# Attention scores: K's low part against Q's high part alone, in passes of 64 rows

## The chip, the cores and the metric

The kernel runs on one core of one Trainium2 chip. The metric is the device time of one execution in microseconds (us); a comparison goes by the median of several executions. TensorE (PE in the profile) multiplies a stationary operand of up to 128 rows and 128 columns, which a load of weights (PEld) puts into its array, with a moving operand that streams through; the rows are the dimension that is summed over. VectorE (DVE), ScalarE (ACT), GpSimd (POOL) and the issuing queue SyncE (SP) work beside it.

## The reference

One step of a hybrid encoder: 1024 prompt tokens and 32 sample tokens of width 1024 go through one layer with a recurrent mixer, then through one layer of sliding-window attention with 16 query heads, 4 key/value heads of 64 dimensions and a learned sink for each head. Only the scores of the second layer are touched by the change:

```python
kb, vb = band(k), band(v)                     # chunks of 64: this one and the two before
s = jnp.einsum('bnqkgd,bnskd->bnkgqs', qb, kb).astype(jnp.float32) * scale
p = sink_softmax(s, sink)                     # max with the sink, exp, divide by the sum
o = jnp.einsum('bnkgqs,bnskd->bnqkgd', p.astype(vb.dtype), vb)
```

All is float32. Outputs are the two streams' activations, the convolution and recurrent states, and K and V rows.

## The kernel before, in words

**High and low parts.** Every product is made from operands that are split into a high part, rounded to the format that TensorE multiplies in one pass (`F32R`), and a low part, the remainder (`split`, L124). Most products are then three passes, high by high, high by low and low by high (`mm3`, L161; `mm3_steps`, L753). The low-by-low product is left out there.

**Scores.** A head has 64 dimensions, so for the scores both parts fit in 128 rows. `q_block` (L905) makes Q of four heads (a group) for a third of the tokens (n = 0, 1, 2: 384, 384 and 288 tokens): `rope` gives the two halves of the dimensions, `halves` splits them into four quarters (high a, high b, low a, low b, 32 rows for each head), they go to `qscr` in device memory and come back as the tile `QU`. Its rows are 32 dimensions each, in the order high a, high b, low a, low b: rows 0-63 hold Q's high part and rows 64-127 its low part, for each of the four heads side by side. `load_kv` (L931) fills `KU` from `kscr`: in `KU[:, 0]` K's high part stands twice, in rows 0-63 and again in rows 64-127, and in `KU[:, 1]` its low part, twice as well. A score block of one head (128 tokens by 256 keys) is therefore two passes of 128 rows: with K's high part, which gives high by high plus low by high, and with K's low part, which gives high by low plus low by low.

**Stages.** For each group g (0 to 3) and each block j of 128 tokens (0 to 7 for the prompt, 8 for the sample) the attention runs in four steps. `stage_s` (L960) makes the scores of four heads in two PSUM banks, two heads in each, and brings them through the mask, the maximum and the exponential into the tile `P` (VectorE at L986, ScalarE at L989). `stage_n` (L993) divides by the sums, `stage_t` (L1003) transposes `P` on TensorE and splits it, and `stage_o` (L1014) multiplies with V (L1019). The loop at L1119 calls `stage_s` of block j+1, `stage_t` of j, `stage_n` of j+1, then six steps of a generator with other products, and `stage_o` of j. These fillers (`fillers`, L1050) are the gate projections `gB` of the group, the Q blocks `rAq` and `rBq` of the next group and, in the last group, the first third of the output projection `obm`.

**What sets the order.** The framework's scheduler orders each engine's instructions by a timing model of its own and by priorities, not strictly as they are written; `pin` marks an instruction that keeps its place in the written order against other marked ones, while unmarked ones can still move in between. Each engine then runs its list in order. Transfers of Q, K, V and weights are issued on SP's queue, in the order of that list as well. In the attention there are three banks for fillers, two for scores (`S`), two for transposes (`T`) and one for `O`.

Of the kernel before, what the change touches and what calls it, by code (L numbers as in the profile page):

```python
# [9 lines left out]
F32 = mybir.dt.float32  # L10
# [7 lines left out]
P = 128  # L18
# [10 lines left out]
NSB = [(0, 384), (384, 768), (768, TOK)]  # L29
# [46 lines left out]
def _trunk(ctx, tc, nc, A):  # L76
    V, S, G = nc.vector, nc.scalar, nc.gpsimd
# [13 lines left out]
    def pin(i, on=True):  # L91
        return tc.keep_in_program_order(i) if on else i

    def bank(name, tag="mm", bufs=None):
        return psum.tile([P, 512], F32, tag=tag, name=name, bufs=bufs or nbank)
# [384 lines left out]
    half = {}  # L480
# [140 lines left out]
    for n in range(3):  # L621
        for m in LATE:
            w = NSB[n][1] - NSB[n][0]
            hl = [late.tile([P, 384], F32R, tag="t", bufs=NT, name=f"y{x}{m}_{n}")[:, :w] for x in "hl"]
# [86 lines left out]
    for n, order in enumerate(orders):  # L711
        zs, acc = {}, []
        w = NSB[n][1] - NSB[n][0]
# [22 lines left out]
    qscr = dram.tile([4, 4, P, TOK], F32, name="qscr")  # L736
    ogscr = dram.tile([6, P, TOK], F32, name="ogscr")

    def att_tile(name, shape, dt, tag, bufs):
        return att.tile([P] + shape, dt, tag=tag, bufs=bufs, name=name)  # L740
# [21 lines left out]
    def rope(n, wA, wB, nm, norm=None):  # L762

        c0, c1 = NSB[n]
        w = c1 - c0
        pa_, pb_ = bank(f"rA{nm}")[:, :w], bank(f"rB{nm}")[:, :w]
        yield from mm3_steps(pa_, wA, x1_of(c0, c1))
        yield
        yield from mm3_steps(pb_, wB, x1_of(c0, c1))
        if norm is not None:  # L770
            norm()
        t = [unit(f"rp{i}{nm}", w=w) for i in range(4)]
        for i, (p, tab) in enumerate(((pa_, cos), (pb_, sin), (pb_, cos), (pa_, sin))):
            V.tensor_tensor(t[i], p, tab[:, c0:c1], op=ALU.mult)
        G.tensor_tensor(t[0], t[0], t[1], op=ALU.subtract)
        G.tensor_tensor(t[2], t[2], t[3], op=ALU.add)
        rope_out[nm] = (t[0], t[2])
        yield
# [7 lines left out]
    def halves(nm, a, b, w):  # L786
        q = quad(f"quad{nm}")
        for i, x in enumerate((a, b)):
            split(q[:, i, :w], q[:, 2 + i, :w], x)
        return q  # L790
# [112 lines left out]
    QU, KU, VU, SG, TT = {}, {}, {}, {}, {}  # L903

    def q_block(g, n):  # L905
        nm = f"q{g}_{n}"
        c0, c1 = NSB[n]
        w = c1 - c0
        yield from rope(n, wts[f"qA{g}"], wts[f"qB{g}"], nm)
        a, b = rope_out.pop(nm)  # L910
        q = halves(nm, a, b, w)
        nc.sync.dma_start(qscr[g].rearrange("x p c -> p x c")[:, :, c0:c1], q[:, :, :w].bitcast(F32))
        QU[g, n] = att_tile(f"Q{g}_{n}", [4, 384], F32R, "Q", 3)
        if n == 2:
            QS[g] = att_tile(f"QS{g}", [4, DEC], F32R, "QS", 2)
        for x in range(4):
            nc.sync.dma_start(QU[g, n][32 * x:32 * x + 32, :, :w].bitcast(F32),
                              qscr[g, x].rearrange("(h d) c -> d h c", h=4)[:, :, c0:c1])
            if n == 2:
                nc.sync.dma_start(QS[g][32 * x:32 * x + 32].bitcast(F32),  # L920
                                  qscr[g, x].rearrange("(h d) c -> d h c", h=4)[:, :, SEQ:])
# [9 lines left out]
    def load_kv(g, n):  # L931
        KU[g, n] = att_tile(f"K{g}_{n}", [2, 640], F32R, "K", 2)
        VU[g, n] = att_tile(f"V{g}_{n}", [5, 128], F32R, "V", 2)
        w = KB1[n] - KB0[n]
        for dup in range(2):
            for half in range(2):
                p0 = dup * 64 + half * 32
                pin(nc.sync.dma_start(KU[g, n][p0:p0 + 32, :, :w].bitcast(F32),
                                      kscr.rearrange("(l f) p c -> p l f c", l=2)[32 * g:32 * g + 32, :, half, KB0[n]:KB1[n]]),
                    g == 0 and n > 0)  # L940
        t0, t1 = KB0[n] // P, KB1[n] // P
        nc.sync.dma_start(VU[g, n][:, :t1 - t0, :].bitcast(F32),
                            vscr.rearrange("t p c -> p t c")[:, t0:t1, g * 128:g * 128 + 128])
# [14 lines left out]
    QS = {}  # L958

    def stage_s(g, j):  # L960

        smp = j == 8
        n = 2 if smp else j // 3
        if (g, n) not in KU:
            load_kv(g, n)
        nm = f"{g}_{j}"
        nh, nk = (1 if smp else 4), (1 if j == 0 else 2)
        t0 = 3 if smp else max(j - 1, 0) - KB0[n] // P
        w = nk * P
        ks = slice(t0 * P, t0 * P + 256)  # L970
        sm = att_tile(f"sm{nm}", [3, 4], F32, "sm", 4)
        nmax, rsum, rl = (sm[:, i, :nh] for i in range(3))
        sk = slice(16 + g, 17 + g) if smp else slice(4 * g, 4 * g + 4)
        msk = smask if smp else mask[:, 256 - w:]

        pt = att_tile(f"P{nm}", [4, 258], F32, "P", 2)
        S.activation(pt[:, :nh, w:w + 1], nsnk[:, sk].unsqueeze(2), AF.Copy)
        for h0 in range(0, nh, 2):
            sb = bank(f"S{nm}_{h0}", "S", 2)
            for h in range(h0, min(h0 + 2, nh)):  # L980
                q = QS[g].rearrange("p h c -> p (h c)") if smp else QU[g, n][:, h, P * j - NSB[n][0]:P * j - NSB[n][0] + P]
                s = sb[:, (h - h0) * 256:(h - h0) * 256 + 256]
                for hl in range(2):
                    pin(nc.tensor.matmul(s, q, KU[g, n][:, hl, ks], start=hl == 0, stop=hl == 1), g == 0 and j == 0)  # L984
            for h in range(h0, min(h0 + 2, nh)):
                V.tensor_tensor_reduce(pt[:, h, :w], sb[:, (h - h0) * 256:(h - h0) * 256 + w], msk,  # L986
                                       -0.125, nsnk[:, sk][:, h:h + 1], op0=ALU.add, op1=ALU.min,
                                       accum_out=nmax[:, h:h + 1])
                S.activation(pt[:, h, :w + 1], pt[:, h, :w + 1], AF.Exp, bias=nmax[:, h:h + 1], scale=-1.0,  # L989
                             accum_out=rsum[:, h:h + 1])  # L990
        return dict(P=pt, nh=nh, nk=nk, t0=t0, n=n, nm=nm, smp=smp, w=w, rsum=rsum, rl=rl)
# [53 lines left out]
    for n in range(3):  # L1045
        for step, _ in enumerate(q_block(0, n)):
            if (n, step) in V_AT:
                v_block(V_AT[n, step], vrows[2])

    def fillers(g):  # L1050
        for m in (2 * g, 2 * g + 1):
            prep_m(f"g{m}", A["w_in_b"][8 + m], KD, 3)
        for n in range(3):
            for m in (2 * g, 2 * g + 1):
                yield from gate_block(m, n)
            if g == 3:
                for m in OG_AT[n]:
                    load_og(m, 0)
        for m in (2 * g, 2 * g + 1):
            del wts[f"g{m}"]  # L1060
        if g < 3:
            for x, nm in enumerate("AB"):
                prep_m(f"q{nm}{g + 1}", A["w_in_b"][2 * (g + 1) + x], KD, 3)
            for n in range(3):
                yield from q_block(g + 1, n)
        else:
            yield from out_b(0)
# [51 lines left out]
    for g in range(4):  # L1119
        fil = fillers(g)  # L1120
        per = PER[g]
        todo = [0, 1, 2]
        st = {0: stage_s(g, 0)}
        stage_n(st[0], False)
        for j in range(9):
            if j < 8:
                st[j + 1] = stage_s(g, j + 1)
            if g == 0 and j == 0:
                for _ in range(2):
                    next(fil)  # L1130
            stage_t(st[j])
            if j < 8:
                stage_n(st[j + 1])
            for _ in range(per - (g == 3 and j > 6)):
                next(fil, None)
            stage_o(g, j, st.pop(j))
            while todo and j >= (2, 5, 8)[todo[0]] and (2 * g + 1, todo[0]) in SG:
                finish_og(g, todo.pop(0))
        if g == 3:
            break  # L1140
        run(fil)
        for n in todo:
            finish_og(g, n)
# [176 lines left out]
```

## Time and profile before

| what | value |
|---|---|
| median of three executions (lowest to highest) | 897.91 us (897.18 to 900.01) |
| the profiled execution, its own time | 896.39 us |
| its span, from first to last instruction | 894.6 us |
| mean granted TensorE clock | 0.997 |
| busy: PE, DVE, ACT, POOL | 881.0, 702.3, 563.6, 211.5 us |
| score passes with Q (L984) | 256, from 541.2 to 798.6 us |

The profile is of one execution. Its span lies inside the execution's own time, which is 1.8 us longer. Records of passes on TensorE overlap, so that what a pass costs is read from the distance between two starts. Rows of the timeline start with the start and the length in us; `x8` at the end means eight instructions in a row, for which the length runs from the first start to the last end. In a form such as `128*128 128x256` the first pair is the rows and columns of the weights, the second the output's partitions and moving columns. Rows of groups end with the busy time, the mean of one in ns, and the idle time before.

### The profile page before, as it was taken

The numbers are of one execution on the slowest core, as the hardware profiler recorded it, in microseconds if no ns is written. First come the engines' busy times: TensorE is split into PE (matmuls) and PEld (weight loads), VectorE is DVE, ScalarE is ACT, GpSimd is POOL, SyncE is SP. The second block draws the span as 40 slices with busy tenths as digits, with TensorE's granted clock in tenths as the row PEclk, the third lists the DMA queues.
The fourth block names the chain that finished last, engine by engine and source line by source line (L and its number), as shares of the span: only waits on it lengthen the run. The fifth ranks groups of instructions, "written<-read, shape, count | busy, mean of one in ns | idle before, by whom it ended". The sixth has DMA issues, their size and how long they took to land.

```text
span 894.6 us, 15865 instructions
## 1 busy us (share of the span) xinstructions
PE 881.0 (98%) x5462; PEld 863.1 (96%) x5462; DVE 702.3 (79%) x1511; ACT 563.6 (63%) x1233; POOL 211.5 (24%) x257
## 2 busy tenths in 40 slices
PE   9999999999999999999998999999999999999996
PEld 8999999999999999999997999999999999999996
DVE  5877878879897654176889847879999999898777
ACT  7848878789354325355675317756767767797652
POOL 5260212134300001124343532113023011002240
PEclk9999999999999999999999999999999999999999
DMA  9533433352544226446455568336448338444984
GB/s 335 199 107 108 118 100 120 110 147 86 182 128 126 91 55 209 136 133 202 145 171 175 190 183 231 97 101 192 115 125 228 99 120 233 118 135 123 300 259 170
DMA packets 96129, 138.76 MB, mean 155 GB/s; under 512 B 16224, under 2 KB 64128, under 8 KB 96048
## 3 DMA queue, kind: packets, MB, share of 16 engines
q1 hardware_dynamic: 86232, 124.24, 45.6%
q10 hardware_dynamic: 9640, 12.96, 4.8%
q8 instruction: 43, 0.70, 0.3%
q0 software_dynamic: 176, 0.54, 0.2%
q14 instruction: 38, 0.31, 0.1%
HBM read 99.54 MB, written 32.13 MB: 147 GB/s over the span
## 4 chain that ended last, share of the span: by engine, by line
PE 66%; DVE 4%; ACT 2%; DMA 2%; issue 1%; POOL 1%; SPq 0%; DVEq 0%; ACTq 0%; POOLq 0%
PE gB L757 10%; PE rAq L757 5%; PE rBq L757 5%; PE obm L757 5%; PE oa L168 5%; PE oa L167 5%; PE oa L169 5%; PE gb L167 4%; PE gb L168 4%; PE gb L169 4%; PE S L984 3%; PE O L1019 3%; PE T L1009 3%; PE ot L757 2%; PE rAk L757 1%
## 5 line engine op out<-in xcount | busy, mean ns | idle before, releaser
L167 PE MATMUL oa<-yh,whi_outa 128*128 128x384 f32 (+1 forms) x264 | 85.8, 326 | 0.0
L168 PE MATMUL gb<-xlo,whi_ina 128*128 128x384 f32 (+1 forms) x264 | 85.6, 324 | 0.0
L167 PE MATMUL gb<-xhi,whi_ina 128*128 128x384 f32 (+1 forms) x264 | 85.3, 323 | 0.1
L169 PE MATMUL gb<-xhi,wlo_ina 128*128 128x384 f32 (+1 forms) x264 | 85.4, 323 | 0.0
L169 PE MATMUL oa<-yh,wlo_outa 128*128 128x384 f32 (+1 forms) x264 | 85.2, 323 | 0.0
L168 PE MATMUL oa<-yl,whi_outa 128*128 128x384 f32 (+1 forms) x264 | 85.1, 323 | 0.0
L675 POOL TENSOR_TENSOR qp<-qp,qp 128x384 f32<-128x384 f32 (+2 forms) x34 | 42.2, 1242 | 178.5 <-ACT qp L673 166.4
L168 PE MATMUL br<-xlo,whi_ina 128*128 128x384 f32 (+1 forms) x240 | 77.7, 324 | 0.0
L167 PE MATMUL br<-xhi,whi_ina 128*128 128x384 f32 (+1 forms) x240 | 77.7, 324 | 0.0
L169 PE MATMUL br<-xhi,wlo_ina 128*128 128x384 f32 (+1 forms) x240 | 77.5, 323 | 0.0
L129 DVE TENSOR_TENSOR wlo_outa<-raw_outa,whi_outa 128x512 fp32r<-128x512 f32 (+1 forms) x60 | 43.0, 731 | 43.1 <-ACT whi_outa L128 42.9
L989 ACT ACTIVATE P<-P,sm 128x257 f32<-128x257 f32 (+1 forms) x132 | 64.3, 489 | 13.1 <-DVE sm L986 12.8
L757 PE MATMUL gB<-xl,whi_g 128*128 128x384 f32 (+1 forms) x192 | 63.1, 329 | 0.0
L757 PE MATMUL gB<-xh,whi_g 128*128 128x384 f32 (+1 forms) x192 | 63.1, 329 | 0.0
L128 ACT ACTIVATE whi_outa<-raw_outa 128x512 fp32r<-128x512 f32 (+1 forms) x60 | 35.5, 594 | 43.4 <-PE oa L168 23.9
L757 PE MATMUL gB<-xh,wlo_g 128*128 128x384 f32 (+1 forms) x192 | 62.8, 327 | 0.0
L986 DVE CUSTOM_DVE_ANT_0 P<-S,mask,nsnk 128x256 f32<-128x256 f32 (+1 forms) x128 | 53.1, 461 | 5.5 <-PE S L984 5.4
L257 DVE SCALAR_TENSOR_TENSOR conv<-ext,pa,conv 128x1060 f32<-128x1060 f32 (+2 forms) x51 | 46.1, 926 | 11.0 <-ACT conv L255 10.5
L167 PEld LDWEIGHTS gb<-xhi,whi_ina 128*128 128x128 f32 x264 | 49.7, 188 | 0.4 <-DVE u L565 0.4
L167 PEld LDWEIGHTS oa<-yh,whi_outa 128*128 128x128 f32 x264 | 49.6, 188 | 0.4
L168 PEld LDWEIGHTS oa<-yl,whi_outa 128*128 128x128 f32 x264 | 49.6, 188 | 0.4
L169 PEld LDWEIGHTS oa<-yh,wlo_outa 128*128 128x128 f32 x264 | 49.7, 188 | 0.0
(316 smaller groups left out, 2889.4 us busy)
## 6 DMA issues: line engine op xcount, KB each, us to landing
raw_ina<-w_in_a SPq DMA_DIRECT2D x44, 256.0 KB, 3.6
raw_outa<-w_out_a SPq DMA_DIRECT2D x40, 256.0 KB, 3.1
raw_ob<-w_out_b SPq DMA_DIRECT2D x32, 256.0 KB, 3.2
qscr<-quadq SPq DMA_DIRECT2D x8, 768.0 KB
Q<-qscr SPq DMA_DIRECT2D x32, 192.0 KB, 3.8
hscr<-u SPq DMA_DIRECT2D x11, 530.0 KB, 2.7
xr<-xr SPq DMA_DIRECT2D x8, 512.0 KB, 8.9
raw_g<-w_in_b SPq DMA_DIRECT2D x16, 256.0 KB, 5.2
```

The source lines that it names most:

```text
L128: pin(S.activation(dst_hi, src, AF.Copy), behind)
L129: (lo_eng or V).tensor_tensor(dst_lo, src, dst_hi.bitcast(F32), op=ALU.subtract)
L167: pin(nc.tensor.matmul(ps, wh, xh, start=i == 0, stop=False), behind and i == 0 or mid and i == n // 2)
L168: nc.tensor.matmul(ps, wh, xl, start=False, stop=False)
L169: nc.tensor.matmul(ps, wl, xh, start=False, stop=last and i == n - 1)
L257: V.scalar_tensor_tensor(c, e[:, c0 + k:c1 + k], pa[:, t, k:k + 1], c, op0=ALU.mult, op1=ALU.add)
L675: G.tensor_tensor(sums[0], sums[0], q, op=ALU.add)
L757: nc.tensor.matmul(ps, l, r, start=c == 0, stop=c == 3 * n - 1)
L984: pin(nc.tensor.matmul(s, q, KU[g, n][:, hl, ks], start=hl == 0, stop=hl == 1), g == 0 and j == 0)
L986: V.tensor_tensor_reduce(pt[:, h, :w], sb[:, (h - h0) * 256:(h - h0) * 256 + w], msk, -0.125, nsnk[:, sk][:, h:h + 1], op0=ALU.add, op1=AL ...
L989: S.activation(pt[:, h, :w + 1], pt[:, h, :w + 1], AF.Exp, bias=nmax[:, h:h + 1], scale=-1.0, accum_out=rsum[:, h:h + 1])
L1009: nc.tensor.transpose(tb[:, h * P:(h + 1) * P], st["P"][:, h, kt * P:(kt + 1) * P], ident)
```

## The change

Three things are changed, all for the 32 stages with prompt tokens.

- In `QU` the four quarters stand in another order for heads 2 and 3 of the group: there rows 0-63 hold the low part and rows 64-127 the high part. For that each of the four loads of a Q block becomes two, one for two heads.
- The pass with K's low part uses only the 64 rows in which Q's high part stands: rows 0-63 for heads 0 and 1, rows 64-127 for heads 2 and 3. Low by low is no longer computed for the prompt. The pass with K's high part stays at 128 rows.
- The eight passes of a stage are written in another order, over both banks: K high of heads 0 and 2, then K low of 0, 2, 1 and 3, then K high of 1 and 3. Heads 0 and 1 write one bank, 2 and 3 the other, so that the passes in a row alternate between banks, and the four of 64 rows are adjacent. All but the first are marked with `pin`. Both banks are taken before the first pass; VectorE's and ScalarE's part follows as before.

```diff
         for x in range(4):
-            nc.sync.dma_start(QU[g, n][32 * x:32 * x + 32, :, :w].bitcast(F32),
-                              qscr[g, x].rearrange("(h d) c -> d h c", h=4)[:, :, c0:c1])
+            for i in range(2):
+                nc.sync.dma_start(QU[g, n][32 * x:32 * x + 32, 2 * i:2 * i + 2, :w].bitcast(F32),
+                                  qscr[g, (x + 2 * i) % 4].rearrange("(h d) c -> d h c", h=4)[:, 2 * i:2 * i + 2, c0:c1])
...
+        sbs = [bank(f"S{nm}_{h0}", "S", 2) for h0 in range(0, nh, 2)]
+        if smp:
+            q = QS[g].rearrange("p h c -> p (h c)")
+            for hl in range(2):
+                nc.tensor.matmul(sbs[0][:, :256], q, KU[g, n][:, hl, ks], start=hl == 0, stop=hl == 1)
+        else:
+            q = QU[g, n][:, :, P * j - NSB[n][0]:P * j - NSB[n][0] + P]
+
+            for h, half in ((0, 0), (2, 0), (0, 1), (2, 1), (1, 1), (3, 1), (1, 0), (3, 0)):
+                r = slice(h // 2 * 64, h // 2 * 64 + 64) if half else slice(0, P)
+                pin(nc.tensor.matmul(sbs[h // 2][:, h % 2 * 256:h % 2 * 256 + 256], q[r, h, :], KU[g, n][r, half, ks],
+                                     start=half == h % 2, stop=half != h % 2), h + half > 0 or g == 0 and j == 0)
         for h0 in range(0, nh, 2):
-            sb = bank(f"S{nm}_{h0}", "S", 2)
-            for h in range(h0, min(h0 + 2, nh)):
-                q = QS[g].rearrange("p h c -> p (h c)") if smp else QU[g, n][:, h, P * j - NSB[n][0]:P * j - NSB[n][0] + P]
-                s = sb[:, (h - h0) * 256:(h - h0) * 256 + 256]
-                for hl in range(2):
-                    pin(nc.tensor.matmul(s, q, KU[g, n][:, hl, ks], start=hl == 0, stop=hl == 1), g == 0 and j == 0)
+            sb = sbs[h0 // 2]
```

How the instructions stand now is shown at three places. First TensorE at the first stage of group 0, j = 0 (S_0_0 is the bank of heads 0 and 1, S_0_2 that of heads 2 and 3; a row's last pair is the output's partitions and the moving columns, the rows of the weights are not in it). Before:

```order
L757 MATMUL rBq_2_6117<-xl_2_5599,whi_qB_4_5947 128x288
L757 MATMUL rBq_2_6117<-xh_2_5598,wlo_qB_4_5948 128x288
L984 MATMUL S_0_0_6212<-K_0_6202,Q_0_6030 128x256 x4
L984 MATMUL S_0_2_6221<-K_0_6202,Q_0_6030 128x256 x4
L757 MATMUL gB_0_6284<-xh_0_4311,whi_g_0_6259 128x384
```

And now:

```order
L757 MATMUL rBq_2_6125<-xh_2_5598,wlo_qB_4_5948 128x288
L990 MATMUL S_0_0_6224<-K_0_6214,Q_0_6030 128x256
L990 MATMUL S_0_2_6225<-K_0_6214,Q_0_6030 128x256
L990 MATMUL S_0_0_6224<-K_0_6214,Q_0_6030 128x256
L990 MATMUL S_0_2_6225<-K_0_6214,Q_0_6030 128x256
L990 MATMUL S_0_0_6224<-K_0_6214,Q_0_6030 128x256
L990 MATMUL S_0_2_6225<-K_0_6214,Q_0_6030 128x256
L990 MATMUL S_0_0_6224<-K_0_6214,Q_0_6030 128x256
L990 MATMUL S_0_2_6225<-K_0_6214,Q_0_6030 128x256
L757 MATMUL gB_0_6296<-xh_0_4311,whi_g_0_6271 128x384
```

The eight passes alternate between the banks; the third to the sixth have 64 rows, and nothing stands between them here. The second place is TensorE at group 0, j = 2, where O is the product with V. Before:

```order
L757 MATMUL gB_0_6328<-xh_0_4550,wlo_g_4_6281 128x384
L984 MATMUL S_2_0_6372<-K_0_6202,Q_0_6030 128x256 x4
L757 MATMUL gB_1_6413<-xh_1_4834,whi_g_0_6259 128x384
L757 MATMUL gB_1_6413<-xl_1_4835,whi_g_0_6259 128x384
L757 MATMUL gB_1_6413<-xh_1_4834,wlo_g_0_6260 128x384
L984 MATMUL S_2_2_6381<-K_0_6202,Q_0_6030 128x256 x4
L1019 MATMUL O_0_6358<-ph_0_0_6302,V_0_6203 128x512
```

And now:

```order
L757 MATMUL gB_1_6425<-xl_1_4921,whi_g_0_6271 128x384
L1028 MATMUL O_0_6370<-ph_0_0_6314,V_0_6215 128x512
L990 MATMUL S_2_2_6385<-K_0_6214,Q_0_6030 128x256
L990 MATMUL S_2_0_6384<-K_0_6214,Q_0_6030 128x256
L990 MATMUL S_2_2_6385<-K_0_6214,Q_0_6030 128x256
L1028 MATMUL O_0_6370<-pl_0_0_6315,V_0_6215 128x512
L990 MATMUL S_2_0_6384<-K_0_6214,Q_0_6030 128x256
L990 MATMUL S_2_2_6385<-K_0_6214,Q_0_6030 128x256
L990 MATMUL S_2_0_6384<-K_0_6214,Q_0_6030 128x256
L990 MATMUL S_2_2_6385<-K_0_6214,Q_0_6030 128x256
```

The scheduler has put an O pass of 128 rows into the run of 64-row passes, between the first pair and the second. The third place is SP's queue at the first Q block. Before:

```order
L912 DMA qscr<-quadq_0_6024 128x4x384
L917 DMA Q_0_6030<-qscr 32x4x384 x4
L841 DMA vscr<-v_6082 128x512
L845 DMA o_v<-vf_6086 128x256
L144 DMA raw_qB_0_6668<-w_in_b 128x512
```

And now:

```order
L912 DMA qscr<-quadq_0_6024 128x4x384
L919 DMA Q_0_6030<-qscr 32x2x384 x8
L841 DMA vscr<-v_6086 128x512
L845 DMA o_v<-vf_6090 128x256
L144 DMA raw_qB_0_6680<-w_in_b 128x512
```

The four loads are eight, each for two heads instead of four, in the same place ahead of V's rows and the next weights.

## The prediction

> **What bounds the kernel now.** I read the busy time by stretch first, then who waits for whom on TensorE, then the groups by shape. The attention runs from about 541 to 812 us.
>
> ```profile
> 541.00:610.00 69.00, 69.00 (x457) 67.64 (x456) 57.17 (x179) 47.81 (x135) 15.50 (x15) 1.00 0.49 143
> 745.00:812.00 67.00, 67.00 (x433) 65.27 (x432) 62.05 (x190) 55.49 (x156) 5.49 (x5) 1.00 0.51 147
> PE obm L757 <- DVE ogl L129: 0.5, 1, 0.5
> L984 PE MATMUL S<-K,Q 128*128 128x256 f32 x256 | 39.9, 282 | 0.0
> ```
>
> The first two rows give, after the length of the stretch, the busy time of PE, PEld, DVE, ACT and POOL, then the granted clock. TensorE is busy for all of it at clock 1.00, VectorE for 83 to 93%. The third row is the only wait of TensorE that the trace shows between 541 and 830 us: 0.5 us, once. So in this part the time is the sum of what the passes occupy on TensorE, and a pass saved or lengthened there changes the end by as much, until another engine falls behind. The 256 score passes carry 282 ns in their records, but records overlap; the price is the distance between starts:
>
> ```profile
> 642.96 1.03 PEld L984 LDWEIGHTS S<-K,Q 128*128 128x128 f32 x8
> 643.09 1.12 PE L984 MATMUL S<-K,Q 128*128 128x256 f32 x8
> 644.04 1.04 PE L1009 MATMUL T<-ident,P 128*128 128x128 f32 x8
> L1009 PE MATMUL T<-ident,P 128*128 128x128 f32 x248 | 36.3, 272 | 0.0
> 645.44 0.39 PE L1019 MATMUL O<-ph,V 128*128 128x512 f32 x1
> 645.67 0.40 PE L1019 MATMUL O<-pl,V 128*128 128x512 f32 x1
> ```
>
> Eight score passes fill 644.04 - 643.09 = 0.95 us, so 0.119 us each; a pass of 512 columns takes 645.67 - 645.44 = 0.23 us. A load of weights begins about when the pass before it starts, so loads hide behind passes: the first load row starts 0.13 us ahead of the first pass.
>
> **The change: what is removed.** Per stage of a group (4 groups, 8 stages with prompt tokens, 32 in all) the eight passes stay eight, and their eight weight loads too. Four of them now use 64 rows each. Fewer rows alone buy nothing:
>
> ```profile
> L446 PE MATMUL gt<-pack,wlo_gate 96*128 96x384 f32 x28 | 9.4, 337 | 0.0
> L169 PE MATMUL gt<-chi,wlo_gate x78: 294/336/342, 66.1 to 214.0; 128*128 128x384 f32 x52, 128*128 128x292 f32 x26
> ```
>
> A pass with 96 rows lasts 337 ns, one with 128 rows 336 ns. The gain exists only if the two passes of a pair, one in rows 0-63 and one in rows 64-127, run at the same time. Then a stage saves two passes, 2 x 0.119 = 0.24 us, and 32 stages 7.6 us. No pass of this trace runs beside another, so the gain is bounded by 0 and 7.6 us. I take the full overlap, because the halves share neither rows nor bank; the other end is a rival.
>
> **What is added: going into 64-row passes and back.** The trace has one place where passes of fewer than 64 rows stand among full ones, the third norm of the input (L329). Its last product is 32 rows high; the first norm has six passes of 128 rows in the same place:
>
> ```profile
> 27.54 0.83 PE L329 MATMUL rs<-diag,ones 128*128 128x128 f32 x6
> 28.12 0.42 PE L167 MATMUL br<-xhi,whi_ina 128*128 128x384 f32 x1
> 28.38 0.33 PE L168 MATMUL br<-xlo,whi_ina 128*128 128x384 f32 x1
> 46.88 0.94 PE L329 MATMUL rs<-diag,ones 128*128 128x128 f32 x6
> 47.75 0.45 PE L167 MATMUL br<-xhi,whi_ina 128*128 128x384 f32 x1
> 48.03 0.33 PE L168 MATMUL br<-xlo,whi_ina 128*128 128x384 f32 x1
> L329 PE MATMUL rs<-diag,ones 32*128 32x32 f32 x2 | 0.4, 282 | 0.0
> L322 DVE TENSOR_SCALAR diag<-ident,stat x9: 224/282/286, 26.3 to 41.8; 128x128 f32<-128x128 f32 x8, 32x32 f32<-32x32 f32 x1
> 43.25 0.63 ACT L128 ACTIVATE whi_ina<-raw_ina 128x512 fp32r<-128x512 f32 x1 [0.73 <-PE br L168]
> ```
>
> From the first of the six to the second pass behind them it is 28.38 - 27.54 = 0.84 us with 128 rows throughout, and 48.03 - 46.88 = 1.15 us where the last two of the six have 32 rows. They are the smaller passes and cost 0.31 us more. Data is no reason: the last diag was written at 41.8 us and the weights behind were split at 43.25 us. So one excursion, in and out, costs about 0.31 us: the array seems to run empty before loads of another height begin. The 32-column passes there empty sooner than the 256-column ones here would: from 256 to 512 columns the distance grows by 0.23 - 0.12 = 0.11 us, so 224 columns are about 0.10 us. My price is 0.31 + 0.10 = 0.41 us for an excursion (bounds: 0, if 64 rows behave unlike 32, and 0.41 with 0.11 on top for every pair, if the second load of a pair waits for the first).
>
> The Trainium skill, TensorEngine Tiling (Array Packing), section Tiling Modes, says that a change of tiling mode drains the engine, while tiles in one mode load and multiply in parallel. The 0.31 us agree with the first half; no run here shows the second. Against the rows stands another rule of the skill, TensorE: Matmul & The Clock Gate, section Part 3: Packing small matmuls: a load overlaps a running matmul only where the rows differ. The load row above starts while a pass on the same 128 rows runs, so the measurement decides; by that rule the second pair's loads would be bare, some 0.1 us more for each of 32 stages, 3 us in all.
>
> **How many excursions.** The written order has the four half passes of a stage in one run, one excursion a stage. In the order that the scheduler made, O or T passes of 128 rows stand inside that run in eight of the 32 stages, nine times in all (in one stage twice): 32 + 9 = 41 excursions, 41 x 0.41 = 16.8 us. In four of the nine places the stranger stands between the two of a pair, which loses 4 x 0.119 = 0.5 us of overlap. With six passes' time for eight, the sum is 16.8 - 7.6 + 0.5 = **+9.7 us**. The profiled execution took 896.39 us, 1.5 us under the median of the three runs shown, so 906.1 us for its like and **907.6 us** for a median; I write 907.
>
> **What costs nothing, and its cover.** Scores of one stage now come later: a bank is whole only with its last pass, at the seventh and eighth position, where the first bank was whole after four.
>
> ```profile
> 647.43 0.48 DVE L986 CUSTOM_DVE_ANT_0 P<-S,mask,nsnk 128x256 f32<-128x256 f32 x1
> 649.25 0.48 DVE L986 CUSTOM_DVE_ANT_0 P<-S,mask,nsnk 128x256 f32<-128x256 f32 x1
> 655.06 0.38 PE L1009 MATMUL T<-ident,P 128*128 128x128 f32 x2
> ```
>
> VectorE comes to the scores of 643.09 only at 647.43, over 3 us after their last pass, and their transposes start at 655.06. That hides the 0.5 us that the first bank is late; uncovered it would be 0.5 us in each of 32 stages, 16 us.
>
> The loads of Q become two for one: 48 more issues on SP's queue, of half the size.
>
> ```profile
> L917 SPq DMA_DIRECT2D Q<-qscr x48: 312/424/1620, 533.0 to 759.2; - x48
> DMA to landing us min/median/max: 2.4/3.8/5.7
> 533.02 1.74 SPq L917 DMA_DIRECT2D Q<-qscr  x4
> 541.25 1.11 PE L984 MATMUL S<-K,Q 128*128 128x256 f32 x8
> ```
>
> Four issues take 1.74 us, so each block of Q and what is queued behind it (weights, K and V of later blocks) is 1.7 us later. The tightest is the first: issued by 534.76, landed 3.8 us later at 538.6, used at 541.25. With eight issues it is 540.3, still 0.9 us ahead; with the slowest landing of 5.7 us the first stage stands 1 us, once. Later blocks have a group's fillers between load and use, and TensorE's one wait of 0.5 us says that weights are early. I put the loads at 0; uncovered, 1.7 us for each of 12 blocks would be 20 us.
>
> **The rivals.**
>
> *Faster: the switch is free.* Where passes with 64 rows enter and leave without emptying the array, only the overlap counts: -7.6 + 0.5 = -7.1 us, 889.3 us for the profiled one, 890.8 us as a median. For it: the only excursion in the trace is of 32 rows, and of passes that are not in the format of the scores. Against it: 0.31 us with nothing else to wait for. It decides below 7.1 / 41 = 0.17 us for an excursion, where the change breaks even.
>
> *No difference: half the switch.* At 0.2 us for an excursion 41 x 0.2 - 7.1 = +1.1 us, 899.0 us. For it: part of the 0.31 us may belong to the short passes themselves.
>
> *Much slower: no overlap.* If the halves of a pair run one behind the other, or their weight loads do (eight loads remain, and the load is what spaces short passes: the eight transposes behind 644.04 are 128 columns wide and still about 0.11 us apart, since 1.04 us are seven distances and a record of 0.272 us), nothing is saved and 41 x 0.41 = 16.8 us are lost: 913.2 us, 914.7 us as a median. For it: every load in the trace starts only at a pass's start. Against it: other rows, other bank.
>
> *A late queue.* SP's longer queue makes TensorE wait for weights; a few of the 12 blocks would add 2 to 5 us to whichever case holds.
>
> **How the numbers follow.** Forecast (overlap with the full switch) 0.52; no overlap 0.17; half the switch 0.13; free switch 0.16; a late queue deciding 0.02. A measurement of this kernel tells about 0.3% (2.7 us, so 895.2 and 900.6 us) from no change. Faster: the free switch and a little of the half one, 0.17; same: most of the half one, 0.12; slower: the rest, 0.71. The range goes from 894 us, above the centre of the free switch, to 915 us, the centre of no overlap. The forecast's own range, with an excursion at 0.31 us (41 x 0.31 - 7.1 = +5.6 us, 903.5 us) and with 0.11 us on top for half of the 64 pairs (3.5 us more than my sum, 911.1 us), is 903 to 911 us.
>
> **What would show it.** Right: the four half passes fill about the time of two (starts of a pair within some 0.02 us), the first half load starts about 0.2 us behind the start of the last full pass instead of with it, and the same at the way back; a stage's eight passes fill 0.95 + 0.17 = 1.12 us where nothing stands inside, and 1.5 us where one does; TensorE stays busy all the time and still waits for nobody. Wrong on the overlap: starts of a pair 0.11 us apart. Wrong on the switch: loads of other heights begin with the pass before them. Wrong on the cover: rows of waits on TensorE for a DMA of Q or of weights, or for P. The forecast falls if stages fill less than 0.95 us.

## The result: 907.0 us, and the profile after

The changed kernel takes 907.01 us (median of four executions, 906.36 to 907.82); the kernel before, run beside it, 897.54 us (median of four, 896.61 to 900.01). The ratio is 1.0102 with the interval [1.0079, 1.0124]: slower by 9.5 us. The forecast was 907.0 us, with a chance of 0.71 for slower.

The profiled execution of the changed kernel is its slowest, 907.82 us with a span of 906.0 us. The scores stand at L990 now. First TensorE's timeline of the first stage (start, length from the first start to the last end, engine and line), cut into pieces so that the eight passes come apart:

```profile
543.42 0.40 PE L990 MATMUL S<-K,Q 128*128 128x256 f32 x2
543.75 0.39 PE L990 MATMUL S<-K,Q 64*128 64x256 f32 x2
543.97 0.28 PE L990 MATMUL S<-K,Q 64*128 64x256 f32 x2
544.18 0.51 PE L990 MATMUL S<-K,Q 128*128 128x256 f32 x2
544.53 0.36 PE L757 MATMUL gB<-xh,whi_g 128*128 128x384 f32 x1
543.75 0.19 PEld L990 LDWEIGHTS S<-K,Q 64*128 64x128 f32 x2
544.18 0.19 PEld L990 LDWEIGHTS S<-K,Q 128*128 128x128 f32 x1
```

- **The pairs overlap.** Two passes of the second pair fill 0.28 us from the first start to the last end, which is the length of one record. Their starts are 0.003 to 0.004 us apart. The two loads of a pair run together as well: two of them fill 0.19 us, the length of one.
- **Going in and coming back each cost a stop.** The two full passes start 0.40 - 0.28 = 0.12 us apart (a record is 0.28 us long), the second at 543.54. The first half load starts only at 543.75, 0.21 us later, where a load before began with the pass ahead of it. The pass that belongs to it has a record of 0.38 us instead of 0.28, since its load lies bare in it: the loads of the second pair start only 0.11 us behind those of the first. On the way back the same: last pair at 543.97, next load at 544.18.
- **The stage fills 1.10 us** up to the next pass (543.42 to 544.53, from starts with more digits), where a stage filled 0.95 before (643.09 to 644.04, with nothing of another kind in it and no wait behind it). Six passes' worth is 6 x 0.119 = 0.71 us, so one excursion costs **0.39 us**. The first stage of before is no such measure: the pass behind it came late there and started at 542.27, 1.02 us after the first.

What TensorE waits for between the first score and the end, in the changed kernel (us in all, times, longest):

```profile
PE obm L757 <- ACT ogh L128: 0.6, 1, 0.6
PE obm L757 <- DVE ogl L129: 0.4, 1, 0.4
```

So here too it is busy throughout, and the loss is in what the passes occupy. Not all of the 11.4 us between the two profiled executions belongs to the change, though: the first score pass already starts 2.2 us later (543.42 for 541.25), behind work that the change doesn't touch (see the last section). From the first score pass to the end of the span it is 906.0 - 543.42 = 362.6 us, and 894.6 - 541.25 = 353.4 us before: **+9.2 us**.

### The profile page after: what moved, and what is told of

It reads as the page before. It is cut to its first block, busy times and chain, and to the rows that moved or that the text cites. A ratio compares the mean times of both kernels' runs of the same rounds, so it can differ in the third digit from the quotient of the medians.

```text
span 906.0 us, 15943 instructions
## 1 busy us (share of the span) xinstructions
PE 890.4 (98%) x5462; PEld 858.9 (95%) x5462; DVE 700.9 (77%) x1511; ACT 563.0 (62%) x1233; POOL 211.3 (23%) x257
```

## Experiments

The theory: each excursion into 64-row passes costs about 0.4 us whatever stands in it, the overlap of a pair gives back 0.119 us, and both add up over 41 excursions and 64 pairs. The rivals: the cost lies in the new order of the passes or in the doubled loads of Q and not in the height; the price goes by pass and not by excursion; the pairs bring nothing.

Each run is compared with executions of the kernel before on the same chip, whose medians went from 897.0 to 898.7 us from group to group.

| run | us, median (executions) | ratio to before | stage, us |
|---|---|---|---|
| before | 897.5 (4) | 1 | 0.95 |
| after | 907.0 (4) | 1.0102 [1.0079, 1.0124] | 1.10 |
| full height, order and loads kept | 900.7 (10) | 1.0032 [1.0020, 1.0045] | 0.95 |
| loads alone | 899.5 (10) | 1.0016 [1.0003, 1.0029] | 0.95 |
| order alone | 897.8 (10) | 1.0000 [0.9985, 1.0014] | 0.95 |
| halves in the same rows | 911.9 (2) | 1.0159 [1.0138, 1.0179] | 1.33 |
| runs unbroken | 904.0 (4) | 1.0075 [1.0057, 1.0093] | 1.10 |
| two excursions a stage | 915.2 (2) | 1.0196 [1.0175, 1.0216] | 1.50 |
| one half pass a stage | 910.2 (2) | 1.0126 [1.0096, 1.0155] | 1.34 |
| all eight passes 64 rows | 903.4 (6) | 1.0062 [1.0036, 1.0087] | 0.87 |

The stage is one with nothing of another kind inside, counted until the weights of the next pass are in.

### The height alone

```diff
-                r = slice(h // 2 * 64, h // 2 * 64 + 64) if half else slice(0, P)
+                r = slice(0, P)
```

> The changed kernel with its order of passes, its doubled loads of Q and its swapped rows for heads 2 and 3, but every pass 128 rows high (K's low part stands twice in the tile, so low by low is computed again). TensorE's order is the changed kernel's, row for row. My theory, that the time goes into entering and leaving 64-row passes: the eight passes of a stage fill 0.95 us again, and the time is that of before, 897 to 899 us. The rival, that the alternating banks, the later first bank or the doubled loads cost it: 905 to 908 us, and stages or waits longer than before.

Measured: 900.7 us, 6.3 us below the changed kernel and 3.0 above the one before. This lies between the two times that were named: most of the loss goes with the height, and 3.0 us do not. TensorE's list is the same as after, pass for pass, so the stages can be set side by side. Clean stages differ by 0.15 us (the first one by 0.09, as its next pass comes late at full height too). One with passes of O inside shows what a stranger costs; first full height, then after:

```profile
586.04 0.76 PE L990 MATMUL S<-K,Q 128*128 128x256 f32 x5
586.64 0.40 PE L1028 MATMUL O<-pl,V 128*128 128x512 f32 x1
586.87 0.39 PE L1028 MATMUL O<-ph,V 128*128 128x512 f32 x1
587.10 0.28 PE L990 MATMUL S<-K,Q 128*128 128x256 f32 x1
587.22 0.40 PE L1028 MATMUL O<-pl,V 128*128 128x512 f32 x1
587.46 0.41 PE L990 MATMUL S<-K,Q 128*128 128x256 f32 x2
587.70 0.71 PE L1018 MATMUL T<-ident,P 128*128 128x128 f32 x5
```

```profile
590.85 0.83 PE L990 MATMUL S<-K,Q 128*128 128x256 f32 x5
591.61 0.50 PE L1028 MATMUL O<-pl,V 128*128 128x512 f32 x1
591.95 0.39 PE L1028 MATMUL O<-ph,V 128*128 128x512 f32 x1
592.26 0.38 PE L990 MATMUL S<-K,Q 64*128 64x256 f32 x1
592.58 0.51 PE L1028 MATMUL O<-pl,V 128*128 128x512 f32 x1
592.92 0.39 PE L990 MATMUL S<-K,Q 128*128 128x256 f32 x2
593.15 0.38 PE L1018 MATMUL T<-ident,P 128*128 128x128 f32 x2
```

1.66 us against 2.30. The run is cut once, between the two of a pair: 0.15 + 0.39 for a second excursion + 0.12 for the lost overlap = 0.66, against 0.64 measured. O's passes behind a switch carry 0.50 instead of 0.40 us, the bare load again. Over all 32 stages the differences add up to +8.5 us: eight with strangers give 4.9, the others 0.15 each. (In two stages it was the full-height run that waited; they are put at 0.15.) The formula 41 x 0.39 - 7.6 + 0.5 gives 8.9. It is a little too high: in the stage with two strangers two pairs are broken, but the two half passes left between the strangers, one of each pair, stand in different rows and run together (the timeline of after):

```profile
582.05 0.38 PE L990 MATMUL S<-K,Q 64*128 64x256 f32 x2
```

So 61 pairs overlap and not 60, and the sum is 41 x 0.39 - 61 x 0.119 = 8.7.

What remained open was the 3.0 us of the full-height run itself. Its profiled execution, at 902.0 us 1.3 above the median of its runs, has even more: from the first score pass to the end of the span 900.2 - 541.12 = 359.1 us, 5.8 more than before. It shows waits that neither kernel has:

```profile
PE O L1028 <- ACT P L979: 1.8, 1, 1.8
PE S L990 <- DVE sm L995: 0.7, 2, 0.4
PE ot L757 <- ACT zb L1113: 0.6, 1, 0.6
```

With the smaller ones TensorE waits 4.3 us there, and 0.5 us before.

### Loads alone, and the order alone

The first is the kernel before with each load of Q cut in two, in the old row order; the second has the new order of the passes at full height, with Q loaded as before.

```diff
-            nc.sync.dma_start(QU[g, n][32 * x:32 * x + 32, :, :w].bitcast(F32),
-                              qscr[g, x].rearrange("(h d) c -> d h c", h=4)[:, :, c0:c1])
+            for i in range(2):
+                nc.sync.dma_start(QU[g, n][32 * x:32 * x + 32, 2 * i:2 * i + 2, :w].bitcast(F32),
+                                  qscr[g, x].rearrange("(h d) c -> d h c", h=4)[:, 2 * i:2 * i + 2, c0:c1])
```

> The kernel before with each load of Q split in two by heads, the rows where they were: the transfers of the change alone. If the doubled loads are hidden, as I predicted: 897 to 898.5 us. If they make the 3 us that remained with the changed kernel's order at full height: 900 to 901 us.

> The kernel before with the changed order of a stage's eight passes, all 128 rows high, Q's loads and rows as before: the order alone. If the order (the first bank whole only with the seventh pass, both banks taken at once, and what the scheduler then moves) makes the 3 us that remained at full height: 900 to 901 us, with waits of TensorE on VectorE and ScalarE in the last group. If it is the loads: 897 to 898.5 us.

With the order alone the run takes 897.8 us, a ratio of 1.0000, known to 1.3 us either way: no cost shows. With the loads alone it takes 899.5 us, between the two times that were named: they cost 0.8 us by the medians and 1.4 by the ratio (0.3 to 2.6 by its interval). The way goes over SP's queue. Behind the last block of Q stand the loads of `ogr`, the attention's output on its way to the last projection. SP's rows for them, before, then with the order alone, the loads alone, and the full-height run:

```profile
762.05 1.79 SPq L639 DMA_DIRECT2D ogr<-ogscr  x4
```

```profile
762.24 1.79 SPq L639 DMA_DIRECT2D ogr<-ogscr  x4
```

```profile
764.32 3.01 SPq L639 DMA_DIRECT2D ogr<-ogscr  x4
```

```profile
764.92 1.79 SPq L639 DMA_DIRECT2D ogr<-ogscr  x4
```

With the doubled loads they are issued 2.3 and 2.9 us later. ScalarE, which works its list in order, stands in front of the split of `ogr`, and behind it the exponentials and the splits of P wait. ScalarE's timeline and waits in the full-height run, then TensorE's:

```profile
770.34 0.52 ACT L128 ACTIVATE ogh<-ogr 128x384 fp32r<-128x384 f32 x1 [5.37 <-DMA ogr<-ogscr]
775.66 0.20 ACT L979 ACTIVATE P<-nsnk 128x4 f32<-128x4 f32 x1
775.94 0.47 PE L1028 MATMUL O<-ph,V 128*128 128x512 f32 x1 [1.83 <-ACT P L979]
```

ScalarE stands for 5.37 us. From 770.34 to 775.86 it works without a gap, and TensorE, which needs its results, stands 1.83 us until 775.94. With the loads alone it is the same chain:

```profile
768.78 0.52 ACT L128 ACTIVATE ogh<-ogr 128x384 fp32r<-128x384 f32 x1 [5.09 <-DMA ogr<-ogscr]
773.84 0.47 PE L1020 MATMUL O<-ph,V 128*128 128x512 f32 x1 [0.82 <-ACT ph L128]
```

With the order alone ScalarE's longest wait for `ogr` is 1.6 us, and TensorE does not stand. The same wait of ScalarE in the kernel before (us in all, times, longest), and then in the changed kernel's timeline:

```profile
ACT ogh L128 <- DMA ogr<-ogscr: 8.0, 4, 3.0
```

```profile
772.26 1.79 SPq L639 DMA_DIRECT2D ogr<-ogscr  x4
775.61 0.52 ACT L128 ACTIVATE ogh<-ogr 128x384 fp32r<-128x384 f32 x1 [2.22 <-DMA ogr<-ogscr]
```

Before, the longest such wait is 3.0 us, and no wait of TensorE follows from it. In the changed kernel it is 2.2 us. ScalarE comes to it at 775.61 - 2.22 = 773.39, which is 8.4 us later than in the full-height run (764.97), while the issue comes 7.3 us later; and the split starts 3.35 us behind the issue instead of 5.42. So 1.1 us of the shorter wait come from the engines' being late, and 2.1 from a quicker transfer, for which the runs show no cause. TensorE doesn't wait there any more. So the costs do not add: loads and order at full height 3.0 us, the excursions in the trace 8.5, together 9.5 and not 11.5 (in the profiled executions 5.8, 8.5 and together 9.2). Loads and order seem to cost more together (3.0 us, 1.8 to 4.0 by the interval) than apart (about 1 and 0); the intervals do not exclude that they simply add, and the runs do not settle it.

### Both halves in the same rows

```diff
-                r = slice(h // 2 * 64, h // 2 * 64 + 64) if half else slice(0, P)
+                r = slice(0, 64) if half else slice(0, P)
```

The diff shows the passes alone; Q keeps the row order and the four loads of before. Every half pass uses rows 0-63, and no two can overlap.

> Q's layout and its four loads as before, the changed order of passes, and all four half passes of a stage in rows 0 to 63, so that no two can run at once. My theory, that the pairs really overlap and this is worth two passes of 0.119 us a stage: half passes start 0.12 us apart, a clean stage fills 1.34 us instead of 1.10, and the time is 907 + 32 x 0.24 = about 914 us. The rival, that the overlap is worth nothing: 907 us.

Measured: 911.9 us. A clean stage fills 1.33 us and the half passes start 0.118 us apart. From the first score pass to the end of the span it is 369.8 us, 7.2 more than after; by the sum the 61 pairs that overlap in after give 61 x 0.119 = 7.3. By the medians it is only 4.9. The profiled executions differ by 3.8 us, because the part ahead of the attention, which is the same code, ran 3.5 us shorter here; that the medians are lower for the same reason is likely, not shown. So the overlap is real, and in the trace it pays the full 0.119 us a pair.

The Trainium skill, TensorE: Matmul & The Clock Gate, section Part 3: Packing small matmuls, gives tiles side by side a span of one pass and about 4 ns for each further tile. By that, an estimate, a pair would cost 0.004 us more than one pass. The trace of after agrees: the starts of its 61 pairs lie 0.002 to 0.004 us apart.

### The runs unbroken

```diff
+                with urgent(300 if half else 0):
                     pin(nc.tensor.matmul(...)
```

The half passes get a higher priority, so that nothing of another kind comes between them: 32 excursions instead of 41, and no broken pair.

> The changed kernel with a higher priority for the four half passes of a stage, so that in the scheduler's order nothing stands between them in any stage: 32 excursions instead of 41, and no broken pair. My theory, 0.35 to 0.40 us for each of the nine extra excursions and 0.12 us for each of four broken pairs: 3.6 to 4.1 us less than the changed kernel, 903 us, still slower than before. The rival, that the strangers inside the run cost nothing and the loss is in the 32 stages alone: 907 us.

Measured: 904.0 us, 3.0 below after where 9 x 0.39 + 0.5 = 4.0 were expected; in the trace, from the first score pass to the end, 2.3. TensorE now waits 1.4 us in the attention and behind it, where it waited 1.0 after (new are 0.4 us for VectorE's sums, 0.3 for a weight's low part and 0.2 for the copy of T); the rest of the difference has no wait to its name. By the medians a stranger is then worth (3.0 - 0.4) / 9 = 0.3 us. That it costs a whole excursion is shown by the stages side by side above, where the list is the same, and not by this time. Even without strangers the change loses 6 us.

### Two excursions a stage

```diff
-            for h, half in ((0, 0), (2, 0), (0, 1), (2, 1), (1, 1), (3, 1), (1, 0), (3, 0)):
+            for h, half in ((0, 0), (2, 0), (0, 1), (2, 1), (1, 0), (3, 0), (1, 1), (3, 1)):
...
-                                     start=half == h % 2, stop=half != h % 2), h + half > 0 or g == 0 and j == 0)
+                                     start=half == 0, stop=half == 1), h + half > 0 or g == 0 and j == 0)
```

> The changed kernel with the passes of a stage in the order K high of heads 0 and 2, K low of 0 and 2, K high of 1 and 3, K low of 1 and 3: the same eight passes, the same pairs, but two excursions a stage where nothing stands inside. My theory, a price per excursion of 0.35 to 0.40 us: 11 to 13 us more than the changed kernel, 918 to 920 us, and a clean stage fills 1.5 us. The rival, a price per half pass or per pair: 907 us.

Measured: 915.2 us, 8.2 above after. I had expected 11 to 13 and had counted wrong: the same strangers now fall between two excursions and cut almost none. There are 65 excursions against 41, and 63 pairs that overlap against 61: 24 x 0.395 - 2 x 0.119 = 9.2 us. From the first score pass to the end it is 371.7 us, 9.1 more than after. The first stage of this run:

```profile
541.69 1.47 PE L990 MATMUL S<-K,Q 128*128 128x256 f32 x8
543.09 0.44 PE L757 MATMUL gB<-xh,whi_g 128*128 128x384 f32 x1
543.37 0.33 PE L757 MATMUL gB<-xl,whi_g 128*128 128x384 f32 x1
543.54 0.34 PE L757 MATMUL gB<-xh,wlo_g 128*128 128x384 f32 x1
```

The stage fills 1.40 us, and the pass behind it 0.28 instead of the 0.17 that the next one takes: 0.11 us of the way back, the bare load, lies in the record of the stranger behind. 1.40 + 0.11 = 1.51, that is 0.71 + 2 x 0.40.

### One half pass a stage

```diff
                 for hl in range(2):
+                    r = slice(0, 64) if hl and h == 3 else slice(0, P)
-                    pin(nc.tensor.matmul(s, q, KU[g, n][:, hl, ks], start=hl == 0, stop=hl == 1), g == 0 and j == 0)
+                    pin(nc.tensor.matmul(s, q[r], KU[g, n][r, hl, ks], start=hl == 0, stop=hl == 1), g == 0 and j == 0)
```

This is the kernel before; only the last of a stage's eight passes has 64 rows (low by low is left out for that head alone).

> The kernel before, except that the last of a stage's eight passes (K's low part with head 3) has 64 rows, so that low by low of that head alone is left out: one half pass a stage, with nothing beside it, and one excursion. My theory, a price of 0.39 to 0.40 us for an excursion, however many half passes are in it: 32 x 0.395 = 12.6 us more than before, about 910 us, though only a quarter of the half passes is left. The rival, that each half pass has its price (a quarter of the 0.39 us): about 901 us.

Measured: 910.2 us, 11.5 above the kernel before by medians and 12.9 from the first score pass to the end (366.3 us). 32 x 0.395 is 12.6. A clean stage fills 1.34 us with a single half pass and 1.33 with four that do not overlap: the price goes by the excursion.

### All eight passes at 64 rows

```diff
-                r = slice(h // 2 * 64, h // 2 * 64 + 64) if half else slice(0, P)
+                r = slice(h // 2 * 64, h // 2 * 64 + 64)
```

Here Q's low part is left out altogether, and a stage is four pairs. The diff shows the rows alone; the passes also carry the higher priority of the unbroken runs, except the first of a stage.

> All eight passes of a stage 64 rows high, so that Q's low part is not multiplied at all (low by high and low by low are left out), four pairs in one excursion, with a higher priority for all but the first pass. In the scheduler's order the first pass stands apart from the other seven in nine stages, so there are 41 excursions, and nine pairs are broken. My theory, 0.395 us for an excursion and 0.119 us won for a pair, so that an excursion pays from its fourth pair on: a clean stage fills 4 x 0.119 + 0.395 = 0.87 us, less than the 0.95 us of before; in all 41 x 0.395 - 119 x 0.119 = +2.0 us over the kernel before, 900 to 902 us with what the doubled loads add, 2 to 4 us under the kernel with the unbroken runs. The rival, that every pass in 64-row mode has a price of its own (0.39 us for four): a clean stage fills 1.2 us or more and the time is 910 us or more.

```profile
698.32 0.34 PE L757 MATMUL gB<-xh,wlo_g 128*128 128x384 f32 x1
698.59 0.74 PE L991 MATMUL S<-K,Q 64*128 64x256 f32 x8
699.26 0.44 PE L757 MATMUL gB<-xh,whi_g 128*128 128x384 f32 x1
699.54 0.34 PE L757 MATMUL gB<-xl,whi_g 128*128 128x384 f32 x1
```

From the full pass ahead to the second one behind it is 1.22 us. Less the two full passes of 384 columns (0.175 each in the trace of before) the stage fills 0.87 us: 4 x 0.119 + 0.39. No other version has a stage below the 0.95 of before; this one is 0.08 us below. The run does not win all the same, and at 903.4 us it misses the 900 to 902 that were named: the first pass of a stage is cut off from the rest nine times (41 excursions and nine broken pairs), so the sum is 41 x 0.39 + 9 x 0.119 - 32 x 4 x 0.119 = +1.8 us, and the run measured 6.5 above its neighbour before. Of the other 4.7 us a good part is TensorE's waits, which are there again as in the full-height run:

```profile
PE obm L757 <- ACT whi_ob L128: 1.8, 1, 1.8
PE ot L757 <- ACT zb L1114: 1.4, 1, 1.4
```

With 0.9 us for `ogl` and P's low part they are over 4 us in this profiled execution, which is the slowest of the six. How much of them is in the median, and that they come by the same way as in the full-height run, is argued, not shown.

## Why the prediction was right, and where it was not

- **Bound by TensorE: right.** TensorE still waits for nobody but twice for a moment in the output projection, and +9.7 us were forecast for the attention where the trace has +9.2.
- **The overlap, 0.119 us a pair: right**, the pairs start within 0.004 us, and taking it away costs 7.2 us in the trace against a term of 7.1. The loads of the second pair are not bare either: they start at 543.86, while the first pair is on, and with four pairs in a row the last ones follow at 0.12 us. (That every load starts only at a pass's start was misread; in the trace of before the load behind a bare one, at 47.85, starts 0.1 us behind the pass of 47.75.)
- **An excursion at 0.41 us: right in size, 0.39, and partly by luck.** That 32-row passes of another format show the price held. The 0.10 us added for the columns stand on a reason that the trace of before does not bear out: behind a pass of 32 columns the next load of another height starts 0.20 us after the pass's start, behind one of 128 columns 0.20 as well, and behind one of 256 columns here 0.21.

```profile
47.21 0.27 PE L329 MATMUL rs<-diag,ones 128*128 128x128 f32 x1
47.41 0.18 PEld L329 LDWEIGHTS rs<-diag,ones 32*128 32x128 f32 x1
47.54 0.27 PE L329 MATMUL rs<-diag,ones 32*128 32x32 f32 x1
47.74 0.19 PEld L167 LDWEIGHTS br<-xhi,whi_ina 128*128 128x128 f32 x1
```

- **Why the 0.31 us there were less than 0.39.** The two 32-row passes stand in for two of 128 columns, at 0.11 us each, and are themselves shorter: their starts are 0.13 us apart, of which 0.11 are the bare load. So they hide part of the price, and a correction was due, but not the one that was made. Here the array emptying alone (0.21 - 0.12 = 0.09 us on each side) is less than half of it; the bare first load (0.11 us on each side) is the larger part, and the prediction did not take it apart. The stage was forecast at 1.12 us and fills 1.10; with a stranger 1.5 us were named, about 0.55 above the 0.95 of full height, and the difference to full height is 0.47 to 0.56 us where no pair is broken, which is the same excursion again.
- **Nine strangers and four broken pairs: right.** The list on the chip is the one that was counted. One excursion each is confirmed by the stages side by side. The broken pairs cost 3 x 0.119 and not 4 x 0.119, since two halves of broken pairs met.
- **The loads of Q at 0: wrong in what covers them.** The step looked at Q's first block, at weights, K and V, and named no wait on ScalarE. The first block was indeed early enough. But behind the last block stand the loads of `ogr`, for which ScalarE already stood 8.0 us before the change, in a row that the prediction did not read. They cost about 1 us by themselves and 3.0 us with the new order. In the changed kernel TensorE does not wait there, partly because the stages around are longer. So the term came out near 0 for a reason that the prediction didn't have.
- **The later first bank at 0: right** within the noise; the order alone measures 1.0000, known to 1.3 us either way.
- **The sum: right, and a little luckily.** 0.39 for 0.41 and 61 pairs make 8.7 us of the 9.7. The stages show 8.5. That 907 was met to the tenth is luck: the executions of the changed kernel alone lie 1.5 us apart. The measured 9.5 leaves about 1 us that could be the loads' remainder or the spread of four executions; the runs do not tell these apart.
- **The rivals.** The free switch falls with the 0.21 us ahead of the first half load, half the switch with 0.39 us, no overlap with 0.004 us. A late queue does not show in the changed kernel, whose TensorE waits neither for Q nor for weights; at full height it does show, by way of ScalarE. No version here beats the kernel before: an excursion needs 0.39 / 0.119 = 3.3 pairs to pay, and a stage has two. Two stages that share one excursion would have four; they need four banks for scores where there are two, and that was not tried.

## What to carry to other kernels

Passes of half height in two halves of the rows do run together, but each visit to them costs about as much as three full passes of 256 columns, so count the excursions in the order that the scheduler really made, not the passes. Look for the price at any place in the trace where a short pass stands among full ones, and take it apart there: the array emptying and a bare load on each side, less what the short passes themselves save. When a change lengthens a queue, look up what the last items behind it are and who already waits for them; such a cost can vanish under a slower engine and come back once that engine gets faster.

## What was not expected of the hardware

A change of height costs 0.2 us on each side here, of which 0.11 is the next load, bare, and the two loads of a pair run together, in 0.19 us. The Trainium skill, TensorEngine Tiling (Array Packing), section Tiling Modes, says that a change of mode drains the engine and that tiles load and multiply in parallel; the prediction could show only the first half, and the trace of after agrees with both.

How long the array takes to empty depends little on short passes. From the start of the last pass to the next one of another height, or its load, it is 0.20 us behind 32 and 128 columns (rows above), 0.21 behind 256 (543.54 to 543.75), 0.27 behind 384 (698.32 to 698.59) and 0.32 behind 512 (591.945 to 592.265). Beyond the time that such a pass takes anyway (0.11, 0.12, 0.17 and 0.23 us from 128 columns on) that is 0.09 to 0.10 us each time.

The spread between executions has at least one place (one kernel alone goes from 896.6 to 900.0 us). At about 480 us, long before the scores, TensorE waits for a norm's sum (3.3 us before, 4.0 after), and behind it the granted clock differs between profiled executions of kernels that have the same code there. Windows of before, then after (length, busy time of PE, PEld, DVE, ACT, POOL, granted clock, DMA share, GB/s):

```profile
480.00:489.00 9.00, 6.05 (x24) 5.45 (x25) 9.00 (x18) 3.85 (x10) 3.92 (x5) 0.81 0.66 187
```

```profile
480.00:489.00 9.00, 4.98 (x15) 4.17 (x14) 9.00 (x18) 3.84 (x10) 4.23 (x4) 0.65 0.71 201
```

The clock is 0.81 before and 0.65 after (1.00 in the run with unbroken runs), and TensorE gets through fewer passes. Set against before, pass for pass, after runs 0.6 us behind at 479 us and 2.1 us at 488: most of the 2.2 us that lie ahead of the attention come from these 9 us, 0.7 of them from the longer wait itself.
